# Half of the cached keys moved beside the delta rule's projection tiles, key pages multiplied in pairs, pooling in stages, and branch B's group norm stepped along with branch A's recurrence

## Chip, core and metric

The kernel is one program on one core of a Trainium2 chip. Times are device microseconds (us), the median of repeated runs; the profile is of one further execution. The core has a matrix engine (TensorE, PE in the rows; its weight loads are PEld), a vector engine (DVE), a scalar engine (ACT), GpSimd (POOL) and a sync engine (SP) that only issues transfers here. Each engine works through its own instructions in order, and so does each engine's DMA queue.

## What is computed

One layer of a hybrid decoder for a prompt of 1024 tokens and 8 decode tokens (1032 columns in all), model width 2048. One input projection feeds four branches of width 512 each, whose gated results go through one output projection and a layer norm.

```python
    proj = jnp.einsum('ntd,de->nte', x, P['w_in'])
    qkv_A, a_A, b_A, z_A, p_B, z_B, qkv_C, f_C, z_C, u_D, z_D = _split_proj(proj)
...
        S = S * jnp.exp(g_last)[..., None, None] + jnp.einsum('nhck,nhcv->nhkv', k_dec, v_new)
...
    yn = ((y - mu_y) * lax.rsqrt(var + GN_EPS)).reshape(N, T, W_BR) * gn_g.astype(F32) + gn_b.astype(F32)
    bonus = jnp.sum(heads(r * k * rho.astype(F32)), axis=-1, keepdims=True) * heads(v)
...
    s = jnp.einsum('nqhd,nshd->nhqs', qb, k) * (HEAD_DIM ** -0.5)
    s = s + jnp.swapaxes(cqb, 1, 2)[..., :, None] - jnp.swapaxes(ck, 1, 2)[..., None, :]
...
    pooled = jnp.concatenate(groups, axis=-1) - u.astype(F32)
    mixed = jnp.einsum('ntgc,gcd->ntgd', pooled.reshape(N, T, POOL_GROUPS, POOL_GW), pool_w.astype(F32))
...
    out = jnp.einsum('nte,ed->ntd', gated, P['w_out'])
    y = _layernorm(ALPHA_DN * x + out, P['ln_g'], P['ln_b'])
```

A is the gated delta rule, worked in chunks of 64 tokens whose state `S` is carried on. B (RWKV-7) carries a state from token to token; its output gets a norm per head (`yn`) and a `bonus`. C is attention with forget gates, in which a decode token sees 4096 cached keys, 32 pages of 128. D takes causal means over 2, 4, 8 and 16 tokens and multiplies each group of 128 columns with a matrix.

## The kernel before

**Tiles.** The input projection is 57 tiles of 128 output columns. `project` (line 343) makes one tile with 16 steps along the 2048 inputs, three column groups of 344 tokens and three matmuls each (`mm3`, line 306: the operands are split in a high and a low part), which is 144 matmuls a tile, written to three banks `pj`. The order of the tiles is `self.seq` (line 1826): a first tile, 16 tiles of B, 16 of A (the delta rule), then four each of C's queries (CQ), D's input and gate (DU, DZ), C's keys, values and gate (CK, CV, CZ).

**Fillers.** All other work of this half of the program is written as generators. `project` calls `fill` (line 315) four times a tile; each call moves each running generator on by its rate, over one or more of its `yield`s. A scheduler then orders the instructions of each engine from this sequence, from priorities and from its own estimate of durations; a matmul that it has put between two others keeps its place on the chip even if its operand comes late. `drain` runs generators to their end without projections beside them.

**Stages of the projections.** In the B stage `prep_b` prepares the recurrence of B. In the A stage (lines 1899 to 1906, 16 tiles) `prep_a` and `operands_a` (lines 399 and 431) do the same for A, with transposes whose results go through two buffers `aost` to memory, by the SP queue; beside it `start_b` inverts B's triangular blocks (`invert`, line 1134) and does the 8 decode tokens of B. In the last stage (`inputs_cd`, 24 tiles) two generators run: `cached` (inversions of A, then `decode_k`, the products of the decode queries with the cached keys, then the softmax) at `RATE_L`, and `recurrent` (`chain_b`, `chain_a`, `branch_d`, `post_chain_b`) at `RATE_R`. Then come C's prompt attention with the cached values, and the output projection.

**Cached keys.** `decode_k` walks over 16 groups of 8 pieces. A piece `dkv` is two pages, 2 x 256 KB, loaded by SP (`pages`, line 916) into one of three buffers, up to two pieces ahead; each is multiplied in four matmuls of 32 output rows (line 997), one for each pair of heads, into four quarters of the bank `k`. The scheduler is free to put each piece anywhere between projection matmuls. An fp32 matmul shows as two instructions in the profile, so a piece is eight.

**Inversion.** After 31 DVE steps the transposed inverse goes to memory (`ut`, line 1173) and back into a block diagonal (`ivB`, line 1176), both by SP, and then into matmuls (line 1182).

**Pooling and norm.** `branch_d` (line 683) handles a group at a time with single buffers: load, shifted adds, mean, load of the gate, SiLU, three matmuls, store. `post_chain_b` (line 1371) reads eight half rows of B's result `YB`, does two head sums by `headsum2` (line 1531, matmuls of `hsl` and `hsh` with `b64r`), and multiplies with the gate; it runs after D, in double buffers.

## Time and profile before

| what | value |
|---|---|
| median of 3 runs (lowest to highest) | 2385.79 us (2385.71 to 2386.83) |
| the profiled execution's own time | 2377.32 us |
| its span, first to last instruction | 2375.6 us |
| PE busy, PEld busy | 2286.3 us (96%), 2032.5 us (86%) |
| DVE, ACT, POOL busy | 1321.3 us (56%), 939.2 us (40%), 336.8 us (14%) |
| moved by DMA | 406.64 MB, 171 GB/s in the mean |
| mean granted TensorE clock | 0.985 of 2.4 GHz |

The profiled execution took 8.5 us less than the median. A span is cut into stretches, and for each the busy time of every engine, the granted clock and the DMA share are read side by side. The matmuls' ends are modelled, so the steps from one start to the next tell more than the durations. Stage borders in this execution: projections to 1709 us, C's attention to 1912 us, output projection to the end.

### The profile page before, as it was taken

Reading aid. Unit: us, or ns where it says so; the run is one execution under the profiler, and the core shown is the slowest. Engines: PE = TensorE matmul, PEld = TensorE weight load, DVE = VectorE, ACT = ScalarE, POOL = GpSimd, SP = SyncE. Lnnn points to the kernel's source line nnn. Section 1 sums busy time; section 2 is a strip of 40 time slices with the busy share of each in tenths; the row PEclk is TensorE's granted clock in tenths of the full one; section 3 lists DMA queues with packets and bytes.
Section 4 is the critical chain, followed back from the end, with each engine's and each line's share of the span. In section 5 each row is a group of like instructions: output and inputs, shape, how many; then the busy total and the mean of one; then the engine's idle time right before and its main releaser. Section 6 shows DMA issues by size and latency. Waiting matters only on the chain. (4 is left out here: it accounts for less than half of the span.)

```text
span 2375.6 us, 47386 instructions
## 1 busy us (share of the span) xinstructions
PE 2286.3 (96%) x17718; PEld 2032.5 (86%) x17718; DVE 1321.3 (56%) x2601; ACT 939.2 (40%) x1853; POOL 336.8 (14%) x432
## 2 busy tenths in 40 slices
PE   8999999999999999899999999999999999999996
PEld 8999999998899999787787777899855579888996
DVE  4665757677676557342222235455587754566544
ACT  5644445434554444121111122454366655220244
POOL 0000000000000000012111112100132111107453
PEclk9999999999999999999999999999999999999998
DMA  6133333455533346768878878743398785686222
GB/s 215 53 102 97 102 87 96 149 110 118 122 81 94 82 110 140 173 174 266 274 263 278 273 263 292 252 156 108 112 265 241 219 301 174 202 313 216 95 89 89
DMA packets 370944, 406.64 MB, mean 171 GB/s; under 512 B 205133, under 2 KB 228606, under 8 KB 369946
## 3 DMA queue, kind: packets, MB, share of 16 engines
q1 hardware_dynamic: 307698, 263.83, 37.6%
q10 hardware_dynamic: 50056, 101.60, 14.3%
q0 software_dynamic: 12960, 38.18, 4.8%
q8 instruction: 140, 2.29, 0.4%
q14 instruction: 90, 0.74, 0.1%
HBM read 318.76 MB, written 84.67 MB: 170 GB/s over the span
## 5 line engine op out<-in xcount | busy, mean ns | idle before, releaser
L308 PE MATMUL pj<-xh,wlo 128*128 128x344 f32 x2688 | 871.5, 325 | 13.5 <-DVE wlo L303 8.6
L309 PE MATMUL pj<-xl,whi 128*128 128x344 f32 x2688 | 868.8, 323 | 0.0
L310 PE MATMUL pj<-xh,whi 128*128 128x344 f32 x2688 | 862.9, 323 | 0.0
L308 PEld LDWEIGHTS pj<-xh,wlo 128*128 128x128 f32 x2688 | 506.4, 189 | 34.2 <-issue 12.1
L309 PEld LDWEIGHTS pj<-xl,whi 128*128 128x128 f32 x2688 | 506.7, 189 | 19.1 <-issue 13.6
L310 PEld LDWEIGHTS pj<-xh,whi 128*128 128x128 f32 x2688 | 505.8, 189 | 16.6 <-issue 13.3
L302 ACT CAST whi<-raw 128x256 fp32r<-128x256 f32 (+1 forms) x504 | 213.1, 424 | 725.2 <-PE pj L310 533.0
L303 DVE TENSOR_TENSOR wlo<-raw,whi 128x256 fp32r<-128x256 f32 (+1 forms) x504 | 237.0, 472 | 364.9 <-ACT whi L302 359.3
L308 PE MATMUL o<-gh,wlo 128*128 128x344 f32 x576 | 185.8, 327 | 2.1 <-ACT gh L1695 1.9
L309 PE MATMUL o<-gl,whi 128*128 128x344 f32 x576 | 186.3, 324 | 0.0
L310 PE MATMUL o<-gh,whi 128*128 128x344 f32 x576 | 185.9, 323 | 0.0
L308 PEld LDWEIGHTS o<-gh,wlo 128*128 128x128 f32 x576 | 109.3, 191 | 23.3 <-DVE y L1720 10.2
L309 PEld LDWEIGHTS o<-gl,whi 128*128 128x128 f32 x576 | 109.4, 190 | 2.4 <-DVE hsl L1536 0.9
L310 PEld LDWEIGHTS o<-gh,whi 128*128 128x128 f32 x576 | 109.5, 190 | 0.8 <-issue 0.8
L365 ACT ACTIVATE stg<-pj 128x344 f32<-128x344 f32 x168 | 74.7, 457 | 75.9 <-PE pj L310 74.7
L997 PE MATMUL k<-dkv,dqb 128*32 128x256 f32 x1024 | 88.2, 392 | 15.3 <-DMA dkv<-in_ck 11.6
L1720 DVE TENSOR_TENSOR y<-y,o 128x344 f32<-128x344 f32 x96 | 47.4, 508 | 47.7 <-PE o L310 47.4
L861 DVE TENSOR_TENSOR cpl<-cpt,cph 128x512 fp32r<-128x512 f32 (+1 forms) x96 | 62.1, 664 | 19.0 <-ACT cph L860 18.3
L1105 PE MATMUL k<-dkv,dpT 128*8 128x512 f32 x512 | 69.0, 614 | 1.2 <-DMA dkv<-in_cv 1.2
L308 PE MATMUL o<-gh,wkl 128*128 128x392 f32 (+2 forms) x192 | 62.8, 327 | 5.0 <-DVE y L1792 5.0
L310 PE MATMUL o<-gh,wkh 128*128 128x392 f32 (+2 forms) x192 | 62.7, 326 | 0.0
L309 PE MATMUL o<-gl,wkh 128*128 128x392 f32 (+2 forms) x192 | 62.4, 325 | 0.0
(607 smaller groups left out, 3345.5 us busy)
## 6 DMA issues: line engine op xcount, KB each, us to landing
dkv<-in_ck SPq DMA_DIRECT2D x256, 256.0 KB
dkv<-in_cv SPq DMA_DIRECT2D x256, 256.0 KB
raw<-in_w ACTq DMA_DIRECT2D x228, 256.0 KB
out_pj<-stg ACTq DMA_DIRECT2D x33, 516.0 KB
bop<-bop SPq DMA_DIRECT2D x16, 1024.0 KB
raw<-in_wo ACTq DMA_DIRECT2D x64, 256.0 KB
aop<-aop SPq DMA_DIRECT2D x16, 768.0 KB
aop<-aost SPq DMA_DIRECT2D x40, 256.0 KB
```

The source lines that it names most:

```text
L302: nc.scalar.copy(hi, raw)
L303: nc.vector.tensor_tensor(lo, raw, hi.bitcast(F32), op=ALU.subtract)
L308: nc.tensor.matmul(ps, lhsT=wlo, rhs=xh, start=start, stop=False)
L309: nc.tensor.matmul(ps, lhsT=whi, rhs=xl, start=False, stop=False)
L310: self.last = nc.tensor.matmul(ps, lhsT=whi, rhs=xh, start=False, stop=stop).ins
L365: self.nc.scalar.activation(dst[:, g * G3:g * G3 + G3], ps[g], func)
L861: nc.vector.tensor_tensor(pl[:, off:], pt[:, off:], ph[:, off:].bitcast(F32), op=ALU.subtract)
L997: nc.tensor.matmul(ps[32 * hp:32 * hp + 32], lhsT=qb[:, hp, b], rhs=kt[:, :, hp], start=b == 0, stop=b == 7)
L1105: mm = lambda i: nc.tensor.matmul(po[32 * i:32 * i + 8], lhsT=pTv[:, c, :, 4 * bg + i], rhs=t[i // 2][:, i % 2], start=False, stop=c == 31)
L1720: nc.vector.tensor_tensor(y[:, s], y[:, s], ps[g], op=ALU.add)
```

## The change

- **Order of the tiles.** The four CQ tiles now come right after B's, ahead of A's; the A stage has 20 tiles and the last one 20.
- **Keys in two halves.** `decode_k` takes `first` and `last`. Groups 0 to 7 run at the end of `start_b`, in the A stage; groups 8 to 15 run in `cached` after the inversions of A. The running sum of the forget gates is carried in a buffer that lives through both. After the first load there is a `yield` of its own ahead of the copies into `dqb`.
- **Pieces in pairs.** Two pieces are fetched, one matmul of the second is issued, and the seven others follow at high priority right behind it (`issue_after`).
- **Pooling in stages.** The inputs and gates of two groups are loaded ahead into double buffers, the mean is written over its input, and the three matmuls of a group come one group later, into banks of two kinds.
- **Norm of B.** `post_chain_b` is moved on once for every step of `chain_a` (and while that waits for the inversions), in single buffers.
- **Softmax.** The transposed weights are stored in two halves. **Rates.** `RATE_R` 1.1 for 1.0, `RATE_L` 1.4 for 1.6.

```diff
@@ -18,13 +18,13 @@
 N = T + NS
 G3 = 344
 GROUPS = (392, 384, 256)
-RATE_R = 1.0
+RATE_R = 1.1
 EARLY = (1,)
 RATE_P = 1
 SPOOL = {0: 99, 1: 99, 2: 0}
 NPOOL = {392: 8, 384: 10, 256: 8}
 VBUFS = 5, 4
-RATE_L = 1.6
+RATE_L = 1.4
 LEAD = 1
 CBANKS = 2, 2, 1
...
@@ -688,12 +688,31 @@
         nc.gpsimd.dma_start(rc, I["rc"])
         bf, bn = (self.t(pool, [128, 4, 8, 15], x, bufs=1) for x in ("dbf", "dbn"))
         nc.gpsimd.dma_start(bf, I["dbf"])
+        U, Z = {}, {}
+
+        def load(gi):
+            if gi < 4:
+                u = U[gi] = self.t(pool, [128, 16 + N], "du", bufs=2)
+                nc.gpsimd.memset(u[:, 0:16], 0.0)
+                nc.gpsimd.dma_start(u[:, 16:], O["pj"][DU + gi])
+                z = Z[gi] = self.t(pool, [128, N], "dz", bufs=2)
+                nc.gpsimd.dma_start(z, O["pj"][DZ + gi])
+
+        def product(gi):
+            z = Z[gi]
+            for g in range(3):
+                s = slice(g * G3, g * G3 + G3)
+                ps = self.ps("bab"[g], (128, G3))
+                nc.tensor.matmul(ps, lhsT=pw[:, gi], rhs=U[gi][:, 16 + s.start:16 + s.stop], start=True, stop=True)
+                nc.vector.scalar_tensor_tensor(z[:, s], ps, self.p("psc", gi), z[:, s], op0=ALU.mult, op1=ALU.mult)
+            nc.gpsimd.dma_start(self.G[12 + gi], z)
+            load(gi + 2)
+        load(0)
+        load(1)
+        yield 1.5
         nc.vector.tensor_copy(bn[:, :, :, 0:14], bf[:, :, :, 1:15])
         for gi in range(4):
-            w = 2 << gi
-            u = self.t(pool, [128, 16 + N], "du", bufs=1)
-            nc.gpsimd.memset(u[:, 0:16], 0.0)
-            nc.gpsimd.dma_start(u[:, 16:], O["pj"][DU + gi])
+            w, u = 2 << gi, U[gi]
             a = self.t(pool, [128, 16 + T], "da", bufs=1)
...
             nc.vector.tensor_tensor(cur[:, 16:32], cur[:, 16:32], rc[:, 16 * gi:16 * gi + 16], op=ALU.mult)
-            yield 1
-            po = self.t(pool, [128, 16 + N], "db" if gi % 2 == 0 else "da", bufs=1)[:, :N]
-            nc.vector.scalar_tensor_tensor(po[:, :T], cur[:, 16:], 1.0 / w, u[:, 16:16 + T], op0=ALU.mult, op1=ALU.subtract)
+            yield 1.5
+
+            nc.vector.scalar_tensor_tensor(u[:, 16:16 + T], cur[:, 16:], 1.0 / w, u[:, 16:16 + T], op0=ALU.mult, op1=ALU.subtract)
             us = u[:, 16 + T:]
             nc.vector.tensor_copy(bn[:, gi, :, 14], us)
             sm = self.t(pool, [128, 8], "dsm", bufs=1)
             nc.vector.reduce_sum(sm, bn[:, gi, :, 15 - w:15] if w < 16 else bn[:, gi], axis=AX.X)
             if w == 16:
                 nc.vector.tensor_tensor(sm, sm, bf[:, gi, :, 0], op=ALU.add)
-            nc.vector.scalar_tensor_tensor(po[:, T:], sm, 1.0 / w, us, op0=ALU.mult, op1=ALU.subtract)
-            z = self.t(pool, [128, N], "dz", bufs=1)
-            nc.gpsimd.dma_start(z, O["pj"][DZ + gi])
-            self.silu(z, self.t(pool, [128, 16 + N], "da" if cur is a else "db", bufs=1)[:, :N])
-            for g in range(3):
-                s = slice(g * G3, g * G3 + G3)
-                ps = self.ps("b", (128, G3))
-                nc.tensor.matmul(ps, lhsT=pw[:, gi], rhs=po[:, s], start=True, stop=True)
-                nc.vector.scalar_tensor_tensor(z[:, s], ps, self.p("psc", gi), z[:, s], op0=ALU.mult, op1=ALU.mult)
-            nc.gpsimd.dma_start(self.G[12 + gi], z)
-            yield 1
+            nc.vector.scalar_tensor_tensor(us, sm, 1.0 / w, us, op0=ALU.mult, op1=ALU.subtract)
+            if gi:
+                product(gi - 1)
+            self.silu(Z[gi], self.t(pool, [128, 16 + T], "da" if cur is b else "db", bufs=1)[:, :N])
+            yield 1.5
+        product(3)
+        yield 1.5
         nc.gpsimd.dma_start(O["obuf"], bn)
 
 
@@ -913,7 +928,7 @@
         nc.gpsimd.dma_start(self.G[8 + hp, :, :T], num)
 
 
...
-    def decode_k(self, **side):
+    def decode_k(self, first, last, **side):
 
 
...
             nc.gpsimd.memset(qb, 0.0)
+            get = self.pages(pool, 3, 2, 8 * last)
+            get(8 * first)
+            yield True
             qf = qb.rearrange("p h b m -> p h (b m)")
             for hh in range(2):
                 r = slice(64 * hh, 64 * hh + 64)
                 nc.vector.tensor_copy(qf[r, :, 8 * hh::33][:, :, 0:8], qs[r])
-            get = self.pages(pool, 3, 2)
-            get(0)
             yield True
-            carry = None
-            for c in range(16):
...
-                        nc.tensor.matmul(ps[32 * hp:32 * hp + 32], lhsT=qb[:, hp, b], rhs=kt[:, :, hp],
-                                         start=b == 0, stop=b == 7)
-                    if b % 2 and b < 7:
+                for b in range(0, 8, 2):
+                    kt = [get(8 * c + b + i).rearrange("p (j h k) -> p j h k", j=2, h=4) for i in range(2)]
+
+                    mm = lambda i, hp: nc.tensor.matmul(ps[32 * hp:32 * hp + 32], lhsT=qb[:, hp, b + i], rhs=kt[i][:, :, hp],
+                                                        start=b == 0 and i == 1, stop=b == 6 and i == 0)
+                    with self.tc.issue_after(mm(1, 0).ins), self.tc.high_priority(offset=AHEAD):
+                        for hp in range(1, 4):
+                            mm(1, hp)
+                        for hp in range(4):
+                            mm(0, hp)
+                    if b < 6:
                         yield True
                 o = 256 * (c % 2)
                 nc.vector.scalar_tensor_tensor(s[:, o:o + 256], ps, 0.125, cum[:, o:o + 256], op0=ALU.mult, op1=ALU.add)
                 if c % 2:
                     nc.gpsimd.dma_start(self.sco[:, 512 * (c // 2):512 * (c // 2) + 512], s)
                 yield True
+            if last < 16:
+                return
             while CK + 3 not in self.done:
                 yield True
 
...
+                pT = self.t(pool, [128, 16, 64], "dpT")
             ps = self.ps("k")
             for i in range(4):
                 o = 512 * (g % 2) + 128 * i
                 nc.tensor.transpose(ps[:, 128 * i:128 * i + 128], sc[g // 2][:, o:o + 128], self.ident)
             src = ps.rearrange("p (g h r) -> p g h r", g=4, h=4)[:, :, :, 0:16]
-            nc.scalar.copy(pT[:, 4 * g:4 * g + 4].rearrange("p g (h r) -> p g h r", h=4), src)
+            nc.scalar.copy(pT[:, 4 * (g % 4):4 * (g % 4) + 4].rearrange("p g (h r) -> p g h r", h=4), src)
+            if g % 4 == 3:
+                nc.gpsimd.dma_start(self.pTd[:, 256 * (g - 3):256 * (g + 1)], pT.rearrange("p g r -> p (g r)"))
             if g % 2:
                 yield True
-        nc.gpsimd.dma_start(self.pTd, pT.rearrange("p g r -> p (g r)"))
         nc.gpsimd.dma_start(self.sco[:, 4096:4097], s0)
 
     def decode_v(self, pool):
...
-                y, z, sq, bv = (self.t(pool, [128, 512], x, bufs=2) for x in ("py", "pz", "ps", "pb"))
+                y, z, sq, bv = (self.t(pool, [128, 512], x, bufs=1) for x in ("py", "pz", "ps", "pb"))
                 nc.sync.dma_start(y, self.YB[hp, :, s])
                 nc.sync.dma_start(z, O["pj"][BT + 4 * hp + 3, :, s])
...
         prep = lambda t: [t + 4 * h + i for h in (0, 1) for i in range(4)] + [t + 8, t + 9, t + 10, t + 12, t + 13, t + 14, t + 11, t + 15]
-        self.seq = [MISC] + prep(BT) + prep(AT) + four(CQ) + four(DU) + four(DZ) + four(CK) + four(CV) + four(CZ)
+        self.seq = [MISC] + prep(BT) + four(CQ) + prep(AT) + four(DU) + four(DZ) + four(CK) + four(CV) + four(CZ)
         with P(name="const", bufs=1) as cp, P(name="psum", bufs=2, space=PSUM) as self.psum0:
...
             self.cached_gates(sp)
             pa = self.post_a(sp, ap, 1.6)
-            self.add(self.start_b(), 1)
-            for t in self.seq[17:33]:
-                self.project(t, raw if (t - AT) % 4 == 3 else pa)
+            self.add(self.start_b(cp), 1)
+            for t in self.seq[17:37]:
+                self.project(t, raw if t < AT or (t - AT) % 4 == 3 else pa)
             self.drain()
 
     def inputs_cd(self, sp):
...
             self.project(t, raw)
         self.drain()
 
-    def start_b(self):
+    def start_b(self, keep):
 
         yield from self.inverses("B")
         with self.tc.tile_pool(reuse_waits="tile", name="smpB", bufs=1) as pool:
             yield from self.sample_b(pool)
+        self.carry = self.t(keep, [128, 1], "dcar")
+        while CQ + 3 not in self.done:
+            yield 1
+        yield from self.decode_k(0, 8)
 
     def cached(self):
         yield from self.inverses("A")
         self.done.add("invA")
-        while CQ + 3 not in self.done:
-            yield 1
-        yield from self.decode_k()
+        yield from self.decode_k(8, 16)
         yield from self.decode_softmax()
         self.done.add("decK")
...
         yield from self.chain_b(**side)
-        while "invA" not in self.done:
-            yield 1
-        yield from self.chain_a(**side)
+        with P(name="post") as pool:
+
+            post = self.post_chain_b(pool)
+            while "invA" not in self.done:
+                next(post, None)
+                yield 1
+            for x in self.chain_a(**side):
+                next(post, None)
+                yield x
+            yield from post
         while DZ + 3 not in self.done:
             yield True
         with P(name="d") as pool:
             yield from self.branch_d(pool)
-        with P(name="post") as pool:
-            yield from self.post_chain_b(pool)
         while "decK" not in self.done or CK + 3 not in self.done:
             yield 1
         self.c0 = self.tc.tile_pool(reuse_waits="tile", name="c0", bufs=1, **side)
```

On PE, in the last stage of the kernel before: two pieces of keys (`k`) of the same group between the projection matmuls (`pj`) of one tile, with a step of A's recurrence (`a_12474`) beside one of them.

```order
L308 MATMUL pj_15348<-xh_17_119,wlo_15151 128x344
L997 MATMUL k_13714<-dkv_13715,dqb_12174 32x256 x4
L309 MATMUL pj_15348<-xl_33_135,whi_15150 128x344
L310 MATMUL pj_15348<-xh_17_119,whi_15150 128x344
L308 MATMUL pj_15349<-xh_17_119,wlo_15151 128x344
L309 MATMUL pj_15349<-xl_33_135,whi_15150 128x344
L310 MATMUL pj_15349<-xh_17_119,whi_15150 128x344
L308 MATMUL pj_15350<-xh_17_119,wlo_15151 128x344
L309 MATMUL pj_15350<-xl_33_135,whi_15150 128x344
L1267 MATMUL a_12474<-aG_12472,aop_12457 64x64 x8
L997 MATMUL k_13714<-dkv_13740,dqb_12174 32x256 x4
L310 MATMUL pj_15350<-xh_17_119,whi_15150 128x344
```

The first is alone between projection matmuls, the second stands behind a step of the recurrence. In the whole program the matmuls of the 128 pieces stand in 113 unbroken stretches: 67 of one whole piece, 13 of two, the rest in parts.

On PE after the change, in the A stage:

```order
L309 MATMUL pj_9642<-xl_37_139,whi_9667 128x344
L310 MATMUL pj_9642<-xh_21_123,whi_9667 128x344
L1012 MATMUL k_9443<-dkv_9710,dqb_8222 32x256 x4
L1012 MATMUL k_9443<-dkv_9689,dqb_8222 32x256 x4
L308 MATMUL pj_9640<-xh_22_124,wlo_9668 128x344
L309 MATMUL pj_9640<-xl_38_140,whi_9667 128x344
```

All pieces stand like this, in 64 stretches of two. Up to the last projection the run of projection matmuls is broken by other matmuls 335 times before and 304 times after. From one pair to the next there are 36 projection matmuls in the median of the A stage and 30 in the median of the last one.

On SP, in the A stage before: B's and A's transfers follow each other (the rows of decay `aobb`, the results `aost` to memory); there are no loads of keys.

```order
L394 DMA out_pj<-stg_7200 128x11
L408 DMA aobb_7733<-brow 64x512 x2
L440 DMA aop<-aost_7440 128x8x64
L440 DMA aop<-aost_7443 128x8x64
L440 DMA aop<-aost_7468 128x8x64
```

On SP, in the A stage after:

```order
L408 DMA aobb_8866<-brow 64x512
L942 ISA
L942 DMA dkv_8576<-in_ck 128x512
L440 DMA aop<-aost_8473 128x8x64
L440 DMA aop<-aost_8476 128x8x64
L942 ISA
L942 DMA dkv_8576<-in_ck 128x512
L942 ISA
L942 DMA dkv_8697<-in_ck 128x512
```

The loads of pages (`dkv`, each after registers are set, the ISA rows) now stand between the stores of `aost` on the same queue, 128 loads in all in this stage.

On PE, in the last stage after: a step of A's recurrence (`aG`), with a head sum of `post_chain_b` in its midst.

```order
L309 MATMUL pj_17236<-xl_44_146,whi_17572 128x344
L310 MATMUL pj_17236<-xh_28_130,whi_17572 128x344
L1291 MATMUL a_14811<-aG_14809,aop_14794 64x64 x3
L1561 MATMUL b_14631<-hsl_14633,b64r_221 128x512
L1562 MATMUL b_14631<-hsh_14632,b64r_221 128x512
L1291 MATMUL a_14811<-aG_14809,aop_14794 64x64 x5
L1012 MATMUL k_16139<-dkv_16161,dqb_14724 32x256 x4
L1012 MATMUL k_16139<-dkv_16140,dqb_14724 32x256 x4
```

The recurrence's matmuls (line 1291) were not mixed with head sums before; those stood after `branch_d`.

## Rows read from the trace of the kernel before

**Rows 1.** The page: busy us, share of the span, instructions of each engine.

```profile
PE 2286.3 (96%) x17718; PEld 2032.5 (86%) x17718; DVE 1321.3 (56%) x2601; ACT 939.2 (40%) x1853; POOL 336.8 (14%) x432
```

**Rows 2.** Stretches: us; busy PE, PEld, DVE, ACT, POOL; clock; DMA share; GB/s.

```profile
560.00:660.00 100.00, 93.91 (x784) 86.78 (x780) 68.04 (x169) 46.13 (x94) 4.59 (x9) 0.98 0.53 116
660.00:960.00 300.00, 299.67 (x2549) 288.33 (x2548) 192.42 (x387) 137.63 (x270) 6.99 (x18) 1.00 0.43 107
960.00:1080.00 120.00, 111.05 (x1258) 97.85 (x1257) 46.76 (x121) 24.50 (x56) 15.30 (x24) 0.96 0.70 174
1080.00:1180.00 100.00, 92.79 (x1063) 73.04 (x1064) 24.00 (x56) 16.11 (x41) 23.71 (x40) 0.98 0.87 269
1180.00:1380.00 200.00, 198.66 (x2401) 159.01 (x2403) 43.33 (x103) 26.01 (x65) 33.08 (x60) 1.00 0.82 271
1380.00:1520.00 140.00, 133.31 (x972) 103.19 (x965) 66.02 (x113) 36.57 (x66) 22.29 (x48) 0.99 0.82 279
1520.00:1709.00 189.00, 187.82 (x1241) 182.99 (x1240) 103.46 (x188) 85.95 (x172) 17.48 (x30) 1.00 0.41 128
```

**Rows 3.** Waits of PE, 490 to 1709 us: us in total, times, longest.

```profile
PE k L997 <- DMA dkv<-in_ck: 11.6, 13, 2.1
PE k L1182 <- DMA ivB<-ut: 8.9, 2, 6.6
PE pj L308 <- ACT stg L365: 3.6, 3, 2.1
PE k L997 <- DVE dqb L968: 2.8, 1, 2.8
PE a L479 <- ACT aost L466: 2.7, 2, 1.9
```

**Rows 4.** Stretches at half clock, columns of rows 2.

```profile
565.60:569.00 3.40, 3.40 (x60) 3.28 (x57) 3.13 (x11) 0.91 (x3) 0.00 (x0) 0.51 0.25 39
...
1418.90:1422.30 3.40, 3.40 (x18) 3.10 (x12) 1.24 (x1) 0.00 (x0) 0.00 (x0) 0.50 0.89 321
```

**Rows 5.** Timeline of PE: start, us, instruction; one piece, then two.

```profile
1266.53 0.32 PE L309 MATMUL pj<-xl,whi 128*128 128x344 f32 x1
1266.68 0.32 PE L310 MATMUL pj<-xh,whi 128*128 128x344 f32 x1
1266.93 0.64 PE L997 MATMUL k<-dkv,dqb 128*32 128x256 f32 x8
1267.50 0.42 PE L308 MATMUL pj<-xh,wlo 128*128 128x344 f32 x1
1267.77 0.32 PE L309 MATMUL pj<-xl,whi 128*128 128x344 f32 x1
...
1208.65 0.32 PE L309 MATMUL pj<-xl,whi 128*128 128x344 f32 x1
1208.90 1.07 PE L997 MATMUL k<-dkv,dqb 128*32 128x256 f32 x16
1209.90 0.42 PE L310 MATMUL pj<-xh,whi 128*128 128x344 f32 x1
1210.16 0.32 PE L308 MATMUL pj<-xh,wlo 128*128 128x344 f32 x1
```

**Rows 6.** Timeline of SP: two of the loads of pieces, columns of rows 5.

```profile
1150.54 0.94 SPq L927 DMA_DIRECT2D dkv<-in_ck  x2
...
1151.73 1.50 SPq L927 DMA_DIRECT2D dkv<-in_ck  x2
```

**Rows 7.** Timeline of PE: the matmuls of these pieces; idle before in brackets.

```profile
1157.11 0.64 PE L997 MATMUL k<-dkv,dqb 128*32 128x256 f32 x8 [0.56 <-DMA dkv<-in_ck]
1159.63 1.08 PE L997 MATMUL k<-dkv,dqb 128*32 128x256 f32 x8 [1.88 <-DMA dkv<-in_ck]
```

**Rows 8.** ACT at line 466 (copies into `aost`), 500 to 960 us: idle until, times.

```profile
  DMA aop<-aost: 11.1, 5
```

**Rows 9.** Waits of PE, whole span: a head sum.

```profile
PE b L1537 <- DVE hsl L1536: 3.5, 1, 3.5
```

More of the change, by code (lines that the diff above doesn't have):

```diff
@@ L913, in c_gate, with pages @@
         nc.gpsimd.dma_start(self.G[8 + hp, :, :T], num)
-    def pages(self, pool, bufs, lead):
+    def pages(self, pool, bufs, lead, end):
         tiles = {}
@@ L929, in get @@
         def get(n):
-            for m in range(n, min(n + lead + 1, 128)):
+            for m in range(n, min(n + lead + 1, end)):
                 if m not in tiles:
@@ L968, in decode_k @@
                 nc.vector.tensor_copy(qf[r, :, 8 * hh::33][:, :, 0:8], qs[r])
-            get = self.pages(pool, 3, 2)
-            get(0)
             yield True
-            carry = None
-            for c in range(16):
+            carry = self.carry
+            for c in range(first, last):
                 if c % 2 == 0:
@@ L1913, in inputs_cd @@
         self.add(self.recurrent(**R), RATE_R)
-        for t in self.seq[33:]:
+        for t in self.seq[37:]:
             self.project(t, raw)
         self.drain()
-    def start_b(self):
+    def start_b(self, keep):
         yield from self.inverses("B")
```

6 lines of the change are left out of this document (1 added, 5 removed).

## The prediction

> **What bounds the kernel now.** First the page: PE is busy for 96% of the span and no other engine for more than 56% [rows 1]. So the time is the sum of what stands in PE's queue, plus what it waits, plus what the half clock costs; work moved on DVE, ACT or POOL matters only where PE waits for it. Second, the stretches of the projections [rows 2]. From 560 to 1709 us PE's idle time is 6.1 + 0.3 + 9.0 + 7.2 + 1.3 + 6.7 + 1.2 = 31.8 us. It lies early in the A stage, at the first inversions of A, and where key pieces run beside B's recurrence and beside the pooling. The long run of A tiles (660 to 960) hardly waits, at a DMA share of 0.43, while the stretches with keys stand at 0.82 to 0.87. PEld falls to 0.73 of the time there, although PE reads as busy: the array is not streaming all of it. Third, whom PE waits for [rows 3]: five rows make 29.6 of these 31.8 us. Fourth, the clock: after some of the waits the granted clock stands at 0.5, 1.2 instead of 2.4 GHz; five such stretches between 490 and 1709 us, of which the first and the last are shown, have 20.4 us, in which about half, 10.2 us, is lost [rows 4]. After the projections the change moves nothing but a few neighbours.
>
> **Part by part.**
>
> *Pairs.* In the timeline a projection matmul follows the next one 0.15 to 0.16 us later [rows 5]. With one piece between them, from the last matmul before it (1266.68) to the second one after (1267.77) it is 1.09 us, of which 0.32 are two ordinary steps: 0.77 us for a piece. With two pieces at once, 1208.65 to 1210.16 is 1.51 us, less 0.32: 1.19 us. Two apart cost 1.54, so each merger saves 0.35 us; the multiplying itself stays, what goes is a turn into the small shape and back. By the order there are 113 stretches before and 64 after, 49 fewer, which would be 17 us. But a piece that stood beside a step of a recurrence paid no turn of its own; counting breaks in the run of projection matmuls instead, over both orders, they fall from 335 to 304, and 31 x 0.35 is 11 us. I take 14, between them, since about half of the merged pieces had projections on both sides.
>
> A rule of the Trainium skill bears on which end is right. "TensorEngine Tiling (Array Packing)", Key Properties, says that a change of tiling mode drains the engine. By it a piece beside a recurrence step, which has another tile shape, pays as well, and the sum would be the 17 us; the rows here show the turn between 128x128 and 128x32 alone.
>
> *Waits for pieces*, 11.6 us in 13 times [rows 3]. A piece issued from 1150.54 was multiplied at 1157.11 after a wait of 0.56 us, one issued from 1151.73 at 1159.63 after 1.88 us [rows 6, 7]: 6.6 and 7.9 us from issue to use at a DMA share of 0.87. After the change, three buffers with pairs leave one piece of the next pair to be loaded from the end of a pair. In the A stage 36 projection matmuls stand between pairs, 36 x 0.16 + 1.19 = 6.9 us: about what the load takes when the queues are full, and the A stage is emptier, 0.43 plus the pages. In the last stage there are 30 and one or two recurrence steps, somewhat more time, at a DMA share like before, because B's norm brings its loads there while pooling no longer overlaps with keys. If a load takes a microsecond less than the gap, most waits go; if one more, 62 pairs wait for a microsecond or so less some slack. I take 10 us (3 to 24): a gain of 1.6.
>
> Here too the Trainium skill has a price: "DMA: Bandwidth & Descriptors", Anatomy of one DMA, gives about 2.0 us and the bytes at 436 GB/s, so 2.6 us for 256 KB as an estimate. The rows say 6.6 and more; by the page the waits for pieces would be nothing after.
>
> *The wait for `dqb`*, 2.8 us: the load of the queries now has a `yield` before its use. It goes: 2.8 (0 to 2.8).
>
> *Inversions of A*, 8.9 us. Same instructions, same trip to memory and back, again beside the first steps of B's recurrence. Two of the four loads of the second one now stand on SP behind a step's loads, which wait for that recurrence. Unchanged (0 to 16).
>
> *Buffers in the A stage*, 3.6 + 2.7 us [rows 3], for `stg` and `aost`. The 128 page loads stand on SP between the stores that free `aost`; behind a page load that waits for its buffer stand those stores, and behind these ACT and DVE with the weights. ACT waited for the stores for 11.1 us in 5 times, of which PE felt 2.7 [rows 3, 8]. The CQ tiles ahead keep the inversions of B away from that work, which speaks for less. I take 7, a loss of 0.7 (4 to 25).
>
> *B's norm beside A's recurrence.* The head sums cost the same matmuls. PE keeps its order, so a head sum whose row comes late holds up the recurrence and the projections behind it. No row shows one there; the nearest is the single 3.5 us wait of a head sum [rows 9]; before, 16 others waited for nothing. I take 2 (0 to 28, 8 half rows at 3.5).
>
> *Pooling in stages.* DVE is at a half there and POOL at a sixth in the stretch from 1380 us [rows 2]; PE's 6.7 us in that stretch are waits for pieces, counted above. Nothing of its own (0 to 1).
>
> *At nothing.* The other queues: the gates' loads of each two groups go by POOL, now half of them in the A stage, where POOL is busy for 7 of 300 us [rows 2], and no longer beside the pooling's loads; B's norm takes two loads a half row on SP and one load and one store on POOL with it. CQ's stores go with their tiles. The rates, the softmax in halves and the carried sum issue the same instructions. If one of these queues is late, it shows in the waits priced above.
>
> *Clock.* With somewhat fewer waits four dips for five: 10.2 to 8, a gain of 2.2 (0 to 8).
>
> Sum: 14 + 1.6 + 2.8 - 0.7 - 2 + 2.2 = 17.9 us. The profiled execution took 2377.3 us and its span 2375.6, the median 8.5 us more; I take that distance as fixed and count from the median: 2385.8 - 17.9 = **2368 us**. The order after C's start changes so little that I put it at nothing, 4 us either way.
>
> **Rivals.**
>
> *The waits vanish (0.18).* The pages get more time and an emptier stage; then pieces, `dqb` and inversions wait for nothing and one dip is left: 17 + 11.6 + 2.8 + 8.9 + 8.5 = 48.8 us, 2337 us. For it: A tiles at a DMA share of 0.43. Against it: the gap of 6.9 us. By "DMA: Bandwidth & Descriptors" of the Trainium skill, with its 2.6 us, this would be the case.
>
> *The pairs wait (0.18).* Load and gap are so close that the waits double to 24 us, with 2 more dips: 12.4 + 3.4 us against what pairs save, so 2368 + 14 is 2382 us, no change that a measurement of this kernel can tell (0.2% is 4.8 us).
>
> *Stores behind pages (0.13), slower.* The A stage has 8 half heads with two ACT copies into `aost` each. If each of the 16 waits long enough for PE to stand 1.9 us, the longest of rows 3, that is 30 us, and with 8 dips of 1.7 us 14 more: 2368 + 44 = 2412 us. It decides from about 10 such stands on. For it: 11.1 us of ACT's waits already without any pages; against it: most of them PE never felt.
>
> **How the numbers follow.** My forecast, anything from 2350 to 2380, has 0.51. Faster by over 0.2% (below 2381.0): 0.50 + 0.18 + 0.06 of the doubled waits = 0.74. Within 0.2%: 0.01 + 0.11 = 0.12. Slower: 0.13 + 0.01 = 0.14. The range leaves out half of the first rival and most of the third: 2338 to 2394 us.
>
> **What would show it.** All matmuls of pieces in rows of 16, and from the last matmul before to the second after 1.5 us. Waits for pieces near 10 us, those in the pooling gone, new ones in the A stage. No wait for `dqb`. One or two waits for `ut` near 1050 to 1150 us. If PE waits for `aost` more than twice in the A stage, or for `hsl` beside A's recurrence, the third rival or my 2 us are at fault. The projections should end about 18 us earlier than 1709. If they do and the median does not follow, C's attention or the output projection has given it back, which I put at nothing.

## The result, and the profile after

The changed kernel takes **2351.36 us**, the median of 4 executions (2341.86 to 2359.30), beside 2386.31 us (2385.71 to 2388.09) for four executions of the kernel before that were timed with it: a ratio of 0.986, 95% interval 0.983 to 0.989, 35 us less. The forecast was 2368 us, 18 less. Here one profiled execution stands for the median less well than it seemed: the profiled execution of before (2377.32 us) was faster than all four of that kernel here, the one of after (2359.30 us) was the slowest of its four. Between those two the difference is 18.0 us. What a typical execution gains beyond that needed a second profile of each kernel (below).

The page of after, the row that answers to [rows 1], and its granted clock in 40 slices:

```profile
PE 2269.9 (96%) x17718; PEld 2034.2 (86%) x17718; DVE 1323.1 (56%) x2603; ACT 945.8 (40%) x1853; POOL 341.0 (14%) x435
...
PEclk9999999999999999999999999999999999999998
```

PE does the same 17718 matmuls in 16.4 us less busy time. The projections end at 1685.7 us, 22.9 earlier than before. The stretches of after, to set beside [rows 2] (us; busy PE, PEld, DVE, ACT, POOL; clock; DMA share; GB/s): A's tiles, the first inversions of A, A's recurrence, the pooling.

```profile
660.00:960.00 300.00, 297.21 (x2719) 268.17 (x2714) 175.19 (x316) 133.35 (x258) 29.87 (x61) 1.00 0.63 184
...
1080.00:1180.00 100.00, 90.23 (x975) 80.25 (x976) 41.54 (x108) 19.27 (x44) 9.15 (x14) 0.95 0.63 162
...
1290.00:1490.00 200.00, 193.43 (x2363) 161.58 (x2362) 87.26 (x168) 64.86 (x129) 32.87 (x53) 0.99 0.83 271
1490.00:1565.00 75.00, 75.00 (x497) 72.44 (x493) 55.78 (x99) 32.55 (x62) 15.03 (x38) 1.00 0.56 193
```

The A stage now carries pages at a DMA share of 0.63 where it had 0.43, and PE still idles only 2.8 us in its 300. The pooling, which no longer has pieces beside it, idles not at all. The idle time has gathered at the inversions of A and beside A's recurrence. PE's waits from 490 to 1686 us, as in [rows 3] (us in total, times, longest):

```profile
PE k L1012 <- DMA dkv<-in_ck: 7.9, 9, 1.7
PE k L1219 <- DMA ivB<-aop: 6.0, 3, 4.3
PE k L1206 <- DMA ivB<-ut: 4.4, 2, 2.9
PE b L1561 <- DVE hsl L1560: 2.8, 5, 1.0
PE pj L308 <- ACT stg L365: 1.7, 2, 1.2
```

Pieces 7.9 for 11.6 us, the inversions 10.4 for 8.9, head sums beside A's recurrence 2.8 (new), `stg` 1.7 for 3.6; the rows for `dqb` and `aost` are gone. ACT still waits for the stores from `aost`, as in [rows 8], but PE never feels it:

```profile
  DMA aop<-aost: 7.6, 6
```

Three stretches at half clock are left where [rows 4] had five:

```profile
1086.70:1093.50 6.80, 4.59 (x17) 4.18 (x18) 0.12 (x1) 0.00 (x0) 0.00 (x0) 0.50 0.65 186
1175.40:1178.80 3.40, 3.40 (x12) 2.66 (x13) 0.00 (x0) 0.00 (x0) 0.00 (x0) 0.50 0.70 181
1294.90:1298.30 3.40, 3.40 (x13) 3.40 (x13) 1.03 (x2) 0.45 (x3) 0.00 (x0) 0.50 0.58 214
```

All pieces come as 64 runs of 16 matmuls. One pair in PE's timeline, beside the two forms in [rows 5]: from the last projection matmul ahead of it (1285.84) to the second behind it (1287.36) it is 1.52 us. Less the 0.32 us of two ordinary steps that is 1.20 us for the pair, against 2 x 0.77 for two single pieces.

```profile
1285.84 0.32 PE L308 MATMUL pj<-xh,wlo 128*128 128x344 f32 x1
1286.10 1.07 PE L1012 MATMUL k<-dkv,dqb 128*32 128x256 f32 x16
1287.10 0.42 PE L309 MATMUL pj<-xl,whi 128*128 128x344 f32 x1
1287.36 0.32 PE L310 MATMUL pj<-xh,whi 128*128 128x344 f32 x1
```

### The profile page after: what moved, and what is told of

It is laid out like the page before. It is cut to its first block, busy times and chain, and to the rows that moved or that the text cites. A ratio compares the mean times of both kernels' runs of the same rounds, so it can differ in the third digit from the quotient of the medians.

```text
span 2357.5 us, 47428 instructions
## 1 busy us (share of the span) xinstructions
PE 2269.9 (96%) x17718; PEld 2034.2 (86%) x17718; DVE 1323.1 (56%) x2603; ACT 945.8 (40%) x1853; POOL 341.0 (14%) x435
## 4 chain that ended last, share of the span: by engine, by line
PE 75%; DMA 13%; DVE 5%; SPq 3%; issue 2%; ACT 2%; ACTq 0%; DVEq 0%; POOL 0%; POOLq 0%
PE pj L308 15%; PE pj L310 15%; PE pj L309 15%; PE o L308 5%; PE o L309 4%; PE o L310 4%; PE k L1012 2%; DMA dkv<-in_ck 2%; PE k L1129 2%; DMA dkv<-in_cv 1%; DMA ostg<-in_xT 1%; DMA py<-yb 1%; PE a L613 1%; DMA cqr<-out_pj 1%; PE b L1561 1%
## 5 line engine op out<-in xcount | busy, mean ns | idle before, releaser
L308 PE MATMUL pj<-xh,wlo 128*128 128x344 f32 x2688 | 869.7, 325 | 11.6 <-DVE wlo L303 8.5
L309 PEld LDWEIGHTS pj<-xl,whi 128*128 128x128 f32 x2688 | 506.9, 189 | 10.4 <-issue 5.7
L303 DVE TENSOR_TENSOR wlo<-raw,whi 128x256 fp32r<-128x256 f32 (+1 forms) x504 | 232.1, 463 | 376.7 <-ACT whi L302 366.5
L876 DVE TENSOR_TENSOR cpl<-cpt,cph 128x512 fp32r<-128x512 f32 (+1 forms) x96 | 67.2, 712 | 18.5 <-ACT cph L875 17.9
L1012 PE MATMUL k<-dkv,dqb 128*32 128x256 f32 x1024 | 68.5, 385 | 8.0 <-DMA dkv<-in_ck 7.9
```

Source lines behind the costliest of these rows:

```text
L303: nc.vector.tensor_tensor(lo, raw, hi.bitcast(F32), op=ALU.subtract)
L308: nc.tensor.matmul(ps, lhsT=wlo, rhs=xh, start=start, stop=False)
L309: nc.tensor.matmul(ps, lhsT=whi, rhs=xl, start=False, stop=False)
L876: nc.vector.tensor_tensor(pl[:, off:], pt[:, off:], ph[:, off:].bitcast(F32), op=ALU.subtract)
L1012: mm = lambda i, hp: nc.tensor.matmul(ps[32 * hp:32 * hp + 32], lhsT=qb[:, hp, b + i], rhs=kt[i][:, :, hp], start=b == 0 and i == 1, stop= ...
```

## The experiments

Every kernel below was timed in several rounds beside the kernel before; single executions of one kernel spread over 8 to 25 us, so ratios carry their intervals.

### Both kernels again

> The changed kernel once more, beside the three others. Theory P (the gain is made of turns of the array that pairs save, about the same in every execution): 2349 to 2353 us, the executions within some 5 us of each other. Rival C (the clock: executions differ by how often PE stands long enough to fall to half clock, and the 35 us of the medians are half luck): the executions spread over 15 us or more, from 2342 to 2360, and the time falls by about as much as the mean granted clock of the execution rises (0.003 more are some 9 us).

Measured: 2347.7 us (2344.8 to 2353.6), ratio 0.984 (0.982 to 0.986). Neither theory has it whole: the median is a little below both, the five executions spread over 9 us, more than theory P allows and less than rival C, and among them the time does not follow the mean granted clock (the fastest had 0.986, the slowest 0.987).

> The kernel before once more, for a second profile of it. If its first profiled execution was a fast one of a wide spread: this one some 2384 to 2390 us, with more us at half clock or more waits than the first. If a profiled execution is always some 8 us faster than the others: 2376 to 2379 us.

Measured: 2380.3 us (2372.6 to 2394.0); against all other executions of the same kernel the ratio is 0.998 (0.996 to 1.000), so about 0.2% is what such a comparison can tell. Its profiled execution took 2394.0 us. Thus the first profile of before was a fast one of a wide spread, not a fixed distance below the median. The waits of PE in this second profile, 490 to 1727 us:

```profile
PE k L997 <- DMA dkv<-in_ck: 12.9, 14, 2.6
PE pj L308 <- ACT stg L365: 8.3, 3, 5.6
PE k L1182 <- DMA ivB<-ut: 8.2, 2, 5.5
```

They are the same waits with `stg` longer, and there are nine stretches at half clock for five. To split a time cleanly I take three parts of the stretch from 490 us to the end of the projections: PE's idle time, what the half clock costs (half of the busy time in it), and the rest of the busy time, the **streamed** time, which is what the matmuls and their turns take at full clock. The number of unbroken stretches of pieces in PE's order stands beside it (the kernels are described below):

| kernel (profiled execution) | stretches | projections end | idle | half clock | streamed |
|---|---|---|---|---|---|
| before | 113 | 1708.6 | 31.9 | 9.1 | 1177.6 |
| before, second profile | 113 | 1727.1 | 39.2 | 20.4 | 1177.5 |
| norm early alone | 107 | 1729.9 | 45.9 | 17.3 | 1176.7 |
| halves alone | 90 | 1784.1 | 109.9 | 12.5 | 1171.7 |
| halves and early norm | 91 | 1686.1 | 21.4 | 5.1 | 1169.6 |
| changed, single pieces | 89 | 1684.8 | 19.9 | 5.1 | 1169.8 |
| changed | 64 | 1685.7 | 28.2 | 5.7 | 1161.8 |
| changed, second profile | 64 | 1685.2 | 25.6 | 7.5 | 1162.1 |
| changed, old pooling and rates | 64 | 1671.0 | 21.1 | 1.7 | 1158.2 |
| changed, one more step for the inversions | 64 | 1687.5 | 26.0 | 11.0 | 1160.5 |
| changed, norm late | 64 | 1758.8 | 97.5 | 12.5 | 1158.9 |
| pairs alone | 64 | 1718.5 | 53.1 | 14.8 | 1160.5 |
| pairs, four buffers | 63 | 1703.3 | 42.9 | 14.5 | 1156.0 |
| changed, all keys late | 60 | 1736.6 | 71.5 | 19.3 | 1155.8 |

The streamed time repeats within 0.3 us in two profiles of one kernel, although these executions were 10 to 17 us apart: the spread is idle time and clock. For the kernel before it lies in the projections; for the changed kernel it lies behind them (671.9 and 661.8 us), where PE idled 49.5 and 44.4 us and the half clock cost 18.5 and 13.2. And the streamed time follows the number of stretches: from 113 to 64 it falls by 17 us (the six profiles with 64 have 1160.3 on average), 0.35 us a stretch. The six range from 1158.2 to 1162.1, so a difference of 4 us between two kernels need not be a matter of stretches.

### Pairs alone

The loop of the pieces from the change put into the kernel before, with three buffers and with four:

```diff
-                for b in range(8):
-                    kt = get(8 * c + b).rearrange("p (j h k) -> p j h k", j=2, h=4)
...
+                for b in range(0, 8, 2):
+                    kt = [get(8 * c + b + i).rearrange("p (j h k) -> p j h k", j=2, h=4) for i in range(2)]
...
```

and, in the second kernel only,

```diff
-            get = self.pages(pool, 3, 2)
+            get = self.pages(pool, 4, 3)
```

> The kernel before, with its pieces of the keys multiplied in pairs and nothing else changed: all 128 pieces still in the last stage of the projections, 64 stretches of pieces for 113, 321 breaks in the run of projection matmuls for 335. Theory P (pairs make the gain, 0.35 us for each merger): 14 to 49 mergers count, 5 to 17 us less, 2369 to 2381 us, middle 2373. Rival M (the moved half of the keys makes the gain, since the waits of the full stage go): within 3 us of 2386, or slower, because with pairs three buffers leave the load of a piece only some 6.5 us and the waits for pieces go from 11.6 us to 24: 2386 to 2394.

Measured: **2401.9 us**, ratio 1.007 (1.004 to 1.009), slower than before by 17 us and more than either theory allowed. The turns were saved all the same (streamed 1160.5, 17.0 us less). This kernel also tells the two counts of the prediction apart: it has 49 stretches fewer than before, but only 14 breaks fewer in the run of projection matmuls (321 for 335), which by 0.35 us would be 5 us. Of the 49 only 16 stood between two projection matmuls; 28 stood beside one and 5 beside none. The waits for pieces did not double:

```profile
PE k L997 <- DMA dkv<-in_ck: 12.5, 13, 2.0
PE a L785 <- ACT ckx L769: 12.3, 1, 12.3
...
PE s L850 <- DVE cqx L832: 7.8, 1, 7.8
PE a L794 <- DVE cm L792: 7.4, 1, 7.4
```

The new waits are the last three, at C's start. The order, which is set when the kernel is built, lays the pairs along 2019 projection matmuls where single pieces took 1520; behind the last piece 576 are left for 1092, so the softmax, the norm and C's first scores come when the projections run out.

> The kernel before with pairs, as in the run of pairs alone, and a fourth buffer for the pieces (three loads ahead for two); all 128 pieces in the last stage. Theory R (room: pairs alone lost because with three buffers the order lays the pieces along 2019 projection matmuls where single pieces took 1520, so that 576 are left behind the last piece for the softmax and C's start, where 1092 were): now 1327 lie along the pieces and 1268 are left, PE's long waits at C's start go, and what pairs save in turns, 50 x 0.35 = 17 us, shows in the time: 2360 to 2370 us. Rival L (the loss is the load on the queues in a stage with all 128 pieces, whatever the order): 2390 to 2405 us, with waits for pieces of 12 us and more. Rival N (pairs save nothing on the chip): 2380 to 2390.

Measured: 2379.7 us (2364.1 to 2388.6), ratio 0.998 (0.996 to 1.001): some 20 us better than pairs with three buffers, no change against before. The long waits for `ckx`, `cqx` and `cm` at C's start are gone and the turns are saved (1156.0), which is theory R. Yet the time is near rival N's and not R's: the pieces, now laid along only 1327 matmuls, wait longer. That the shorter run of matmuls makes them wait fits, but is not separated from the fourth buffer itself.

```profile
PE k L997 <- DMA dkv<-in_ck: 21.6, 17, 2.3
```

So in these two kernels pairs by themselves save their turns and lose them again, in one at C's start, where few matmuls are left behind them, and in the other in waits for loads.

### The changed kernel with single pieces

The loop of the pieces as before, with its `yield` after every second piece:

```diff
-                for b in range(0, 8, 2):
...
+                for b in range(8):
...
```

> The changed kernel with the pieces one by one as before (89 stretches of pieces for 64, 309 breaks in the run of projection matmuls for 304), all else as in the changed kernel. Theory P: slower than the changed kernel by 5 to 25 times 0.35, 2 to 9 us, 2353 to 2360 us. If the pairs alone were the 14 us of the sum, 2365. Rival M (the moves make the gain): within 2 us of the changed kernel, 2349 to 2353.

Measured: 2355.7 us (2346.9 to 2365.8), ratio 0.988 (0.985 to 0.990): about 8 us slower than the changed kernel, with overlapping intervals, and 7.7 us more streamed (1169.8 for 1162.1). This is the time of theory P. In streamed time rival M fails, since the pairs do count, but it is right on the whole: 29 of the 37 us are there without them.

### Halves and norm, each alone and both

The halves alone: CQ ahead of A's tiles, pieces 0 to 63 in the A stage (`start_b`), the others in the last one (`cached`). The norm alone: stepped next to A's recurrence. Both edits also give the norm's tiles the single buffers of the change, and the first stores the softmax in two halves. Of each the lines that matter:

```diff
-        self.seq = [MISC] + prep(BT) + prep(AT) + four(CQ) + four(DU) + four(DZ) + four(CK) + four(CV) + four(CZ)
+        self.seq = [MISC] + prep(BT) + four(CQ) + prep(AT) + four(DU) + four(DZ) + four(CK) + four(CV) + four(CZ)
...
+        yield from self.decode_k(0, 8)
...
-        yield from self.decode_k()
+        yield from self.decode_k(8, 16)
```

```diff
-        yield from self.chain_a(**side)
...
+            for x in self.chain_a(**side):
+                next(post, None)
+                yield x
```

> The kernel before with the keys in two halves alone: the queries' tiles ahead of A's, pieces 0 to 63 beside the A stage and 64 to 127 in the last one, the queries' load a step ahead of its use; single pieces, pooling, the place of the norm and the rates as before. 90 stretches of pieces for 113, 1440 projection matmuls left behind the last piece for 1092. Theory H (the halves make most of the gain): 23 x 0.35 = 8 us of turns, 2.8 of the queries, some 4 of waits for pieces, some 10 at the end of the stage and in the clock: 2357 to 2365 us. Rival S (the halves are worth only their turns and waits, the rest comes from the norm, the pooling and the rates): 2368 to 2376 us.

Measured: **2470.7 us**, ratio 1.037 (1.034 to 1.040), with 2382.8 us for before: 88 us slower. Both theories fall. PE's waits from 490 us on, and the stretch in which most of them lie:

```profile
PE b L1541 <- DVE hsl L1540: 78.7, 12, 12.6
PE a L785 <- ACT ckx L769: 13.4, 1, 13.4
```

```profile
1625.00:1735.00 110.00, 22.64 (x55) 13.62 (x56) 43.50 (x66) 36.47 (x53) 6.97 (x13) 0.50 0.23 72
```

What PE waits for there are the head sums of B's norm (`hsl`), looked at in the next kernel.

> The changed kernel with the norm and gate of B behind the pooling again, nothing beside A's recurrence. Theory P (the norm beside the recurrence costs PE a few head sums that come late, 2.8 to 4.1 us in the two profiles of the changed kernel, and gives nothing): 2343 to 2348 us, and the waits for the head sums beside A gone. Rival E (moved early, it empties the end of the last stage, where the softmax and C's start need DVE and ACT): 2353 to 2365 us, with PE's waits at C's start grown by 5 us or more.

Measured: **2443.8 us**, ratio 1.025 (1.023 to 1.027): the changed kernel loses some 95 us when its norm goes back behind the pooling. Rival E has the place right and the size wrong by far. PE's waits from 490 to 1760 us, the stretch in which they lie, and the head sums of two half rows in it, one matmul for either half of a sum:

```profile
PE b L1561 <- DVE hsl L1560: 63.6, 11, 12.6
PE a L800 <- ACT ckx L784: 13.4, 1, 13.4
```

```profile
1617.00:1709.00 92.00, 17.85 (x41) 10.53 (x42) 37.61 (x57) 30.83 (x45) 6.10 (x12) 0.50 0.24 75
```

```profile
1627.02 0.80 PE L1561 MATMUL b<-hsl,b64r 128*128 128x512 f32 x1 [12.16 <-DVE hsl L1560]
1627.61 0.63 PE L1562 MATMUL b<-hsh,b64r 128*128 128x512 f32 x1
1631.12 0.79 PE L1561 MATMUL b<-hsl,b64r 128*128 128x512 f32 x1 [2.87 <-DVE hsl L1560]
1631.71 0.63 PE L1562 MATMUL b<-hsh,b64r 128*128 128x512 f32 x1
1644.91 0.79 PE L1561 MATMUL b<-hsl,b64r 128*128 128x512 f32 x1 [12.57 <-DVE hsl L1560]
```

For 92 us PE does little but head sums, one half row every 17.9 us, and the granted clock stands at 0.50 (1.2 GHz) throughout. Before, the first head sum found 1152 projection matmuls left and the last one 576. Here the first finds 720, and from the eighth on only 288, those of the last two tiles, which stay behind. The four tiles of queries that went ahead of A are 4 x 144 = 576 matmuls, some 92 us at 0.16 us each. They are missing as **cover**, that is, as work that PE can do while a chain of small steps runs on the other engines.

That is one half of it; the other is that both these kernels have the single buffers that the change gives the norm's tiles. In the bare stretch the load of the next half row is issued at 1640.12 us, when the last step on the one before has ended, and ACT waits for it:

```profile
1640.12 0.33 SPq L1401 DMA_DIRECT2D py<-yb  x1
1643.51 0.62 ACT L1559 CAST hsh<-py 128x512 fp32r<-128x512 f32 x1 [4.87 <-DMA py<-yb]
```

With DVE busy for 37.61 and ACT for 30.83 of these 92 us, the half rows follow each other without overlap. From the first to the fifteenth head sum before takes 103 us and this kernel 140. How much of the loss is the missing cover and how much the missing second buffer was not separated; a run with the queries early, the norm late and two buffers would do it.

> The kernel before with the norm and gate of B beside the recurrence of A, and nothing else of the change: all keys in the last stage, single pieces, the queries' tiles there too. 107 stretches of pieces for 113, 1102 projection matmuls behind the last piece for 1092. Theory B (balance: the early norm only pays for the cover that moving the queries' tiles takes from the last stage; where that cover is still there, PE had hardly waited for the norm, 3.5 to 4 us, and nothing is to be had): 2376 to 2386 us. Rival G (the early norm is a gain by itself, because C's start no longer has the norm's work on DVE and ACT beside it): 2355 to 2370 us. Rival 0 (head sums beside the recurrence hold PE up): 2390 us and more.

Measured: 2390.5 us, ratio 1.004 (1.002 to 1.005): 8 us slower, above theory B and at rival 0 in size, but not by its cause. The head sums beside the recurrence cost PE 0.4 us. (Before, PE waited 0 and 0.5 us for the norm's head sums; the 3.5 us of [rows 9] belong to a head sum at 1925 us, behind the projections.) What grew are the waits for pieces (11.6 and 12.9 us in the two profiles of before):

```profile
PE k L997 <- DMA dkv<-in_ck: 24.1, 18, 3.6
```

The norm's loads now stand on the same queue beside those of the pieces, from 1184 to 1367 us. But only 7.0 us of these waits lie there (0.8 and 3.0 in the profiles of before), and 11.1 us lie behind them (6.3 and 3.9). So the loads can explain half of the growth; the rest stays open.

> The kernel before with the two parts together that each lost by itself: the keys in two halves (plus 86 us alone) and the norm of B beside A's recurrence (plus 8 alone); single pieces, pooling and rates as before. Theory K (cover: the halves take the queries' four tiles, 576 projection matmuls, from beside the norm, the early norm moves to where matmuls are left, so the two losses cancel): 2348 to 2360 us, no long waits for the norm's head sums, and against the changed kernel without its pooling and rates some 8 us more, in turns that single pieces take. Rival A (parts add up): 2383 + 86 + 8, some 2475 us. Rival Z (pairs are needed too): 2380 us and more.

Measured: **2352.3 us** (2347.8 to 2355.8), ratio 0.986 (0.983 to 0.988), theory K. Two parts that lose 88 and 8 us gain 35 together. Its waits for pieces:

```profile
PE k L997 <- DMA dkv<-in_ck: 6.7, 6, 2.7
```

The waits for pieces are small although the norm's loads stand beside half of them, and PE waits for none of the norm's head sums: the first of them finds 1788 projection matmuls left and the last 1228. This kernel has the norm's single buffers too, so with enough matmuls beside it the norm does not need the second.

### All keys late

The changed kernel with `decode_k(0, 16)` in the last stage, the queries still ahead of A and the norm early.

> The changed kernel with all 128 pieces in the last stage of the projections, in pairs, behind the inversions of A; the queries' projections stay early, and the norm of B beside A's recurrence. Theory P: no loss from the turns (60 stretches, 283 breaks for 304, which by 0.35 us would even be 7 us less), a little for waits in the fuller stage: 2345 to 2358 us. Rival M: the waits for pieces come back (11.6 us and more for 7.9) and the last stage has too little beside which to lay the pieces: 2362 to 2380.

Measured: 2434.9 us, ratio 1.020 (1.018 to 1.022), worse than rival M's 2362 to 2380. Waits for pieces are 17.0 us, and behind the last piece only 144 projection matmuls remain, so the softmax stands bare:

```profile
PE k L1079 <- DVE dsc L1071: 18.8, 1, 18.8
PE k L1012 <- DMA dkv<-in_ck: 17.0, 10, 4.7
PE a L800 <- ACT ckx L784: 12.1, 1, 12.1
```

### The small edits, and a step more for the inversions

Old pooling and old rates in the changed kernel:

> The changed kernel with the pooling of before (one stage after another, its gates loaded late) and the rates of before, all else as in the changed kernel. 310 breaks in the run of projection matmuls for 304, 64 stretches as there. Theory P (nothing is in them): 2345 to 2352 us. Rival T (the recurrence, the norm, the pooling and C's start make one chain, and after the change the last stage has no cover to spare, so a longer pooling shows at its end): 2356 us and more, with waits of PE for the pooling's tiles or at C's start.

Measured: 2346.6 us (2340.8 to 2353.7), ratio 0.986 (0.984 to 0.988): theory P, nothing measurable is in them. Against the kernel of halves and early norm this one differs by the pairs alone. The medians are 6 us apart, but the two ratios, each against its own executions of before, are the same. Its streamed time is 11.4 us less, while behind the projections it idled 50.6 us for 44.2. So how much of the pairs' turns reaches the end, between 0 and 8 us, stays open.

```diff
             nc.sync.dma_start(BD[32 * q:32 * q + 32, :, 32 * q:32 * q + 32], self.UT[q].rearrange("c p i -> p c i"))
         yield True
+        yield True
```

and the same behind the loads of the second matmuls:

> The changed kernel with one more step between the two loads of each inversion and the matmuls that use them (a second yield at either place), so that by the order 93 projection matmuls stand between the two halves of A's first inversion for 44, but 42 for 55 in its second. Theory W (the 8 to 10 us that PE waits for these loads go with the matmuls laid between): the waits for the inversions fall to 3 to 6 us and one dip of the clock goes, 2338 to 2346 us. Rival Q (the loads are late because 16 of them are issued one after another on SP behind other work, and the order answers by laying less between elsewhere): waits as before, 2345 to 2353 us.

Measured: 2352.2 us, ratio 0.987 (0.985 to 0.989), no change against the changed kernel, which is rival Q's time. The waits for the inversions fell to 5.9 us, as theory W has it, but no dip of the clock went (four, 11.0 us), and other waits took their place:

```profile
PE b L1563 <- DVE hsl L1562: 7.0, 6, 1.9
PE a L1366 <- issue: 4.4, 1, 4.4
PE k L1012 <- DMA dkv<-in_ck: 3.7, 5, 1.8
PE k L1221 <- DMA ivB<-aop: 2.7, 1, 2.7
```

PE idled 26.0 us in the projections, as without the edit (28.2 and 25.6). No version tried here is measurably faster than the changed kernel.

## Why the prediction was right, and where not

Between the first profiles the terms were forecast as 17.9 us and came to 18.1: streamed 15.8, idle 3.7, clock 3.4, less 4.8 given back behind the projections. Between the second profiles the sum is 45.1: streamed 15.4, idle 13.6, clock 12.9, and 3.2 more behind the projections. The streamed part is steady; waits and clock are what varies from one execution to the next. That the first sum meets the forecast almost exactly is luck: idle and clock gave 7.1 us where 3.9 was forecast, turns 15.8 where 14 was, and 4.8 went back in a part that was put at nothing. By the medians the kernel gained 35 us, about twice the forecast, and 2351 us lies at the lower end of the forecast's 2350 to 2380.

- *The baseline* is the step that failed for the size. "I take that distance as fixed": it is not. The profiled execution of before had five dips of the clock in the projections where another had nine, so the waits and the clock that the change removes were undervalued: 1.6 + 2.8 - 0.7 - 2 + 2.2 = 3.9 us. Idle time and clock together fell by 7.1 us between the first profiles and by 26.5 between the second; the medians, 35 us less some 15 streamed, give about 20.
- *Pairs*, 14 us forecast (11 to 17): 15.4 to 15.8 streamed. The mechanism and the price of 0.35 us hold; of the two counts, stretches (49, so 17 us) was the right one, breaks in the run of projections (31) not. The kernel with pairs alone shows it best: 49 stretches, but only 14 breaks fewer, and 17.0 us. "TensorEngine Tiling (Array Packing)", Key Properties, of the Trainium skill says that a change of tiling mode drains the engine, by which a piece beside a recurrence step pays as well; the trace agrees, with 17.0 us for 49 stretches. But the term was given to the wrong edit: half of it comes without pairs, since in two halves single pieces already stand in 89 to 91 stretches for 113.
- *Waits for pieces*, 10 us forecast: 7.9 and 6.1. That the gap between pairs decides, on which the estimate rested, is not borne out: single pieces in the changed kernel wait as long (7.9), and in two halves without pairs it is 6.7. Waits like those of the rival "pairs wait" came where all 128 pieces stand in the last stage, with pairs (12.5, 17.0 and 21.6) and without (24.1). The sum of that rival is also short: with its two dips and without the forecast's gain of clock it comes to some 2388 us, not 2382. "DMA: Bandwidth & Descriptors", Anatomy of one DMA, of the Trainium skill gives its 2.0 us and 436 GB/s for transfers that GpSimd issues; the loads of the pieces are SP's. The estimate of 2.6 us from it does not hold for them: the rows have 6.6 and 7.9 us from issue to use, and by it the waits that are left would not be there.
- *`dqb`*, 2.8 to 0: as forecast (in the kernel of halves and early norm 1.3 us remain with the same `yield`). *Inversions*, unchanged at 8.9: 10.4 and 8.2. *Clock*, 8 us: 5.7 and 7.5.
- *`stg` and `aost`*, 7 us forecast, a loss of 0.7: 1.7 in both profiles, where before had 6.3 and 10.3. So this term has the wrong sign, and between the second profiles its 8.6 us are the largest share of the idle time gained. The order of the tiles is what goes with it: in all nine profiles with the queries ahead of A's tiles, the one with all keys late included, PE waits at most 2.6 us for `stg` up to 1680 us and never for `aost`; in the five others 3.6 to 8.5 and 2.0 to 3.3. The page loads did not hold up the stores in a way that PE felt, and the rival "stores behind pages" has nothing left.
- *Norm beside A*, 2 us: the head sums waited for 2.8 and 4.1 us. The number holds, the reasoning is the gap of the prediction. It priced what the early norm costs and never what it pays for. "CQ's stores go with their tiles" stands under "at nothing", while the four tiles take some 92 us of matmuls from beside the norm; with the norm left where it was, in its single buffers, this change is 60 us slower than before. That rival was not on the list.
- *Pooling and rates*, nothing: none was measured. *Behind C's start*, 4 either way: a loss of 4.8 between the first profiles and a gain of 3.2 between the second; the two profiles of the changed kernel alone differ by 10 us there.

## What to carry to other kernels

A matmul that is moved to another stage takes cover from the stage it leaves: count the matmuls that stay beside each serial chain, and name what stands bare when they run out. Parts of one change need not add up: here pairs, halves and the early norm each lose alone, and the last two together make most of the gain. So a sum over parts has to be worked out for the order of matmuls that they give together. One profile of a kernel whose executions spread by 1% is a poor baseline for waits and clock; its streamed time is a good one.

## What the hardware showed that was not expected

A stretch of pieces more, that is a turn of the array into 128x32 and back, costs 0.35 us in the mean: 17 us for 49, over profiles that differ by up to 4 us at the same count. It counts also where a projection matmul stands on one side only: with pairs alone 17.0 us went for 49, of which 16 stood between two of them and 28 beside one. Stretches with none on either side are too few (13 before, 8 in the changed kernel) to be priced by themselves. Executions of one kernel differ by 20 us (before: 2372.6 to 2394.0 in one series) with equal streamed time in the two that were profiled; these differ by their waits and by how many stretches at 1.2 GHz come with them (five and nine in the projections). When PE did little but head sums, busy for 17.9 of 92 us, the granted clock stayed at 0.50 (1.2 GHz) for all of it.
